# Two MLPs by seven products: where a group's first copy-out and three of its sums stand in the queues of ScalarE and VectorE

## The chip, the core and the metric

The kernel runs on one core of a Trainium2 chip. The metric is the device time of one execution in microseconds (us), the median of several runs; smaller is better.

## The reference, cut to what matters

Two layers over 512 tokens of width 1024, all in float32. Layer 0 mixes with stick-breaking attention, layer 1 with a gated linear recurrence; behind each mixer stands an MLP. The change touches the two MLPs alone:

```python
D_MODEL, SEQ, D_FF = 1024, 512, 4 * 1024

def squared_relu_mlp(h, w1, w2):
    u = jax.nn.relu(h @ w1)          # 512 x 1024 by 1024 x 4096: "up"
    return (u * u) @ w2              # 512 x 4096 by 4096 x 1024: "down"

for layer in range(2):
    x = x + mixer(rms_norm(x, norm_mix[layer]))
    x = x + squared_relu_mlp(rms_norm(x, norm_mlp[layer]), mlp_w1[layer], mlp_w2[layer])
return rms_norm(x, norm_final)
```

## The kernel before, in words

**Operands.** Every float32 operand of a matrix product is cut into two halves of a shorter format, and TensorE multiplies three times (high by high, low by high, high by low). The high half is a cast on ScalarE (`wh` for weights, `bh` and `sh` for activations, 128x1024 a weight block), the low half the difference between raw data and high half, a subtraction on VectorE (`wl`, `bl`, `sl`). So each weight block costs a DMA, a cast on ScalarE and a subtraction on VectorE before TensorE may use it.

**Seven products.** The hidden width of 4096 is taken in four quarters `q4` = 0 to 3. Quarter 0's upward product is done plainly (`squared`). From quarter 1 on the upward product is done in two groups `p` = 0 and 1, each a 2x2 block product with seven block products in place of eight, in the order P1, P5, P6, P3, P7, P2, P4; the downward product of a quarter has the same seven, twice each (`g` = 0 and 1). One product of one group is a step; a loop of a quarter has 28 steps, 14 upward and 14 downward. An upward step is 24 matmuls of 256 columns, a downward step 12 of 512.

Four of the seven need a sum of two weight blocks: VectorE adds for P5 and P6 (`b<-b,b`), a DMA of GpSimd that adds while it writes does it for P7 and P4 (line 1053). P3's weights are a plain block (`b22`).

**Banks.** An upward group sums in three banks of PSUM: P1, P6, P7 and P4 in the first, P5 and P3 in the second, P2 in a third. A partial sum has to be copied out by ScalarE before the next product adds to that bank: P1's copy (`u<-ps_...`, COPY) stands between P1 and P6, which are two steps apart, P5's between P5 and P3. The copies, combined on VectorE, become the four blocks of `u`. After relu and square, `split` cuts them into halves, and `sums` makes four sums of the four blocks, each from the one before, for the downward products.

**Order.** TensorE's order is the list of steps. ScalarE's and VectorE's work of the MLPs is held to the order in which the code records it (`Ordered`): between step `i` and step `i + 1` stands `leave(i)`, the work that follows product `i`, and in it `prepare(i + 4)`, which makes the weights' halves for a later step (`make`, `operand`). There are four buffers for `wh` and `wl`, taken in turn. `operand`, `sums`, `split` and `leave` record through `self.A` (ScalarE) and `self.V` (VectorE); all these instructions carry the helper's line, L765, in the profile. Matmuls of upward steps are L976, of downward ones L1071.

When an upward group's P1 is about to run, the step before it, which is P4 of the group before (a downward one for `p` = 0, the upward group 0 for `p` = 1), calls `prepare` for this group's P3. So the halves of P3's weights are recorded ahead of the copy of P1. Behind P4 of group 0, relu and square of the last block come first, then P3's halves, then

```python
                elif name == "P4":
                    self.sums(p, slice(0, 2))
```

Of the kernel before, what the change touches and what calls it, by code (L numbers as in the profile page):

```python
# [61 lines left out]
def hybrid_encoder(  # L62
# [234 lines left out]
    def home_tile(tag, n, name):  # L297
        return home.tile([P, S], F32, tag=tag, name=name, bufs=n)

    with ExitStack() as actx:  # L300
# [4 lines left out]
        later = sp.tile([P, S], F32, tag="later", name="later")  # L305
# [94 lines left out]
        sums = hp.tile([P, S], F32, tag="early", name="ssq")  # L400
        odd = hp.tile([P, S], F32, tag="ks", name="odd", bufs=1)
        sqs = [sums, odd, *(sc[:, :S] for sc in scans)]
        sqs += [work.tile([P, S], F32, tag=tag, name="sq") for tag in ("sq", "sq", "r")]
        others = {getattr(mybir.EngineType, e) for e in ("Activation", "DVE", "Pool", "SP")}
        with tc.manual_schedule(engines=others):
# [14 lines left out]
            for kind, c in START:  # L420
                if kind == "x":
                    halves("mix0", c, xcs[c])
                elif (kind, c) == ("q", 0):
                    parts[0][3](c, None)
                elif kind != "s":
                    parts["qknm".index(kind)][3](c)
                else:
                    A.activation(sqs[c], xcs[c], AF.Square)
                    if c:
                        V.tensor_tensor(sums, sums, sqs[c], ALU.add)  # L430
# [268 lines left out]
        steps = chain(*(g for g, _ in fill))  # L699
# [6 lines left out]
        for i in range(n_fill):  # L706
# [5 lines left out]
            if i == LATE:  # L712
                x = [home_tile(tag, n, "x") for tag, n in HOMES[:7]]
# [61 lines left out]
    class Mlp:  # L775
# [104 lines left out]
            (2, 3, 2, ALU.subtract), (3, 0, 3, ALU.subtract), (0, 2, 0, ALU.subtract), (1, 0, 1, ALU.add),  # L880
        )

        def sums(self, p, i):

            u = self.u[p]
            for out, x, y, op in self.SUMS:
                self.V.tensor_tensor(u[:, i, out, :], u[:, i, x, :], u[:, i, y, :], op)

        def xa(self, block, k):
# [219 lines left out]
        def run(self, first, between, end):  # L1109
# [5 lines left out]
            steps = []  # L1115
# [5 lines left out]
            units, ws, sums, us = {("down", 0): first}, {}, {}, {}  # L1121

            def place(i):

                return (i + self.STEPS // 2) % self.STEPS
# [8 lines left out]
            def add(i, ahead=1):  # L1134

                if i >= len(steps) or i in done or steps[i][3] not in ("P5", "P6"):
                    return
                *what, name = steps[i]
                far = what[0] == "down" and (name, what[2]) in FARS
                if ahead > (5 if far else 2 if name == "P5" else what[0] == "up"):  # L1140
                    return
                if steps.index((*what, {"P5": "P1", "P6": "P5"}[name])) in made:
                    done.add(i)

                    self.added(unit(i), name, far=far)

            def make(i):
                if i >= len(steps):
                    return
                name = steps[i][3]  # L1150
                kind, q4, p, name = steps[i]
                at = 0
                if kind == "up":
                    at = self.OPEN_AT if (p, name) == (0, "P1") else UP_AT
                ws[i] = made[i] = self.operand(self.source(unit(i), name), at)

                for before, x in (("P5", "P7"), ("P6", "P4")):
                    if name == before:
                        self.added(unit(i), x)

            def prepare(i):

                if i < len(steps) and steps[i][0] == "up":

                    if steps[i][3] == "P7" or self.layer and steps[i][1:] == (1, 0, "P4"):
                        return
                if i - 1 in range(len(steps)) and i - 1 not in made and i > 2:
                    make(i - 1)
                if i < len(steps) and steps[i][0] == "down":
                    add(i, 0)  # L1170
                    if waiting and place(i) in (20, 22, 23):
                        self.split_slot(*waiting.pop(0))
                make(i)
                for n in range(i + 1, i + 6):
                    add(n, n - i)

            def last_sums(u, which):
                for to, a, b, how in which:
                    self.V.tensor_tensor(u[to], u[a], u[b], how)

            def load(i):
# [18 lines left out]
                elif at == 25 and q4 < NQ - 1:  # L1200
                    self.load(units["up", q4 + 1], (1, "b12"), (1, "b22"))

            def leave(i):

                ahead = i + 4
                if i < 0:
                    return
                kind, q4, p, name = steps[i]
                bank = sums[kind, q4, p if kind == "up" else 0][self.PRODUCTS[name][3]]
                if kind == "down":  # L1210
                    if p:
                        for n in range(2):
                            self.collect(name, n, bank[n])
                    prepare(ahead)
                    if q4 == 0:

                        k = {19: 2, 20: 2, 24: 3, 25: 3}.get(place(i))
                        if k:
                            (self.sums_of_x if place(i) in (19, 24) else self.halves_of_sums)(k)
                        if place(i) == 26:  # L1220
                            self.replace()
                    return
                u, three = us[p], bank.rearrange("p (i n) -> p i n", i=2)
                keep = {"P1": 0, "P6": 1, "P5": 2, "P7": 3}.get(name)
                if keep is not None:

                    self.A.copy(u[keep], three)
                at, x, y, op = {
                    "P3": (1, three, u[1], ALU.subtract),
                    "P7": (2, u[2], u[3], ALU.subtract),  # L1230
                    "P2": (0, u[0], three, ALU.add),
                    "P4": (3, three, None, None),
                }.get(name, (None,) * 4)
                if op:
                    self.V.tensor_tensor(u[at], x, y, op)
                if name == "P4":
                    self.A.activation(u[3], three, AF.Relu)
                    self.square(u[3])
                    if p:
                        last_sums(u, self.SUMS[:2])  # L1240
                if later:
                    later.pop()()
                prepare(ahead)
                if op:
                    def rest(u=u, at=at):
                        self.A.activation(u[at], u[at], AF.Relu)
                        self.square(u[at])
                        if p:
                            self.split_slot(p, u[at], at)

                    if p and name == "P3":
                        later.append(rest)
                    else:
                        rest()
                    if name == "P2" and not p:
                        self.split(p, slice(0, 2), slice(0, 3), slice(0, 3))
                elif name == "P4" and p:
                    last_sums(u, self.SUMS[2:3])
                    self.split_slot(p, u[2], 5)
                    last_sums(u, self.SUMS[3:])  # L1260
                    waiting[:] = [(p, u[j], 3 + j) for j in (0, 1, 3)]
                elif name == "P4":
                    self.sums(p, slice(0, 2))
                elif name in ("P5", "P6") and p:
                    n = ("P5", "P6").index(name)
                    self.split(0, n, slice(0, 4), slice(3, 7))

            waiting, later = [], []
            make(0)
            add(1)  # L1270
            make(1)
# [11 lines left out]
            for i, (kind, q4, g, name) in enumerate(steps):  # L1283
                load(i)
                leave(i - 1)
                if i == len(steps) - 2:
                    break
                if kind == "down":
                    self.part(sums.setdefault((kind, q4, 0), {}), name, g, ws.pop(i))
                    continue  # L1290
                if name == "P1":
                    us[g] = self.slots_of(g)
                banks = sums.setdefault((kind, q4, g), {})
                to = self.PRODUCTS[name][3]
                new = to not in banks
                if new:
                    banks[to] = self.bank()
                self.up(name, ws.pop(i), banks[to], new)
# [492 lines left out]
```

## Time and profile before

| | |
|---|---|
| median of 3 runs | 1037.46 us (1037.34 to 1038.66) |
| the profiled execution's own time | 1038.87 us |
| its span, first to last instruction | 1037.2 us |
| mean granted TensorE clock | 0.999 |
| busy: TensorE matmul, weight loads | 1023.4 us, 890.5 us |
| busy: VectorE, ScalarE, GpSimd | 858.2 us, 701.7 us, 172.3 us |

In the profile's names PE is TensorE's matmuls, PEld its weight loads, DVE VectorE, ACT ScalarE, POOL GpSimd, SP the queue that issues most DMAs. Each row of a timeline gives the start in us from the span's start, the time that the row took, engine, line, operation, output and input tiles; in square brackets stands the idle time of the engine before it and what ended it. Matmuls overlap, so that a matmul's own time is longer than the spacing of their starts; gaps are read from starts and from the weight loads' waits. The layers' MLP loops lie at about 290 to 563 us and 757 to 1030 us of the span.

### The profile page before, as it was taken

To read this page: it belongs to the slowest core of one execution; us is meant where nothing else is said; L and a number is where in the kernel's file an instruction comes from. 1 tells how busy PE (TensorE), PEld (TensorE's weight loads), DVE (VectorE), ACT (ScalarE), POOL (GpSimd) and SP (SyncE) were. 2 spreads that over 40 slices of the span, in tenths; PEclk is the share of its full clock that TensorE was granted. 3 is DMA by queue.
4 is the path that set the end of the run, shared out by engine and by line. 5 is a ranking of instruction groups with operands and counts; after the bars stand their busy time and mean duration, and the time that the engine had idled before them with its cause. 6 is when DMAs were issued, how large, how long until landed. Compare 5 with 4: busy or idle time off the path is not lost.

```text
span 1037.2 us, 15857 instructions
## 1 busy us (share of the span) xinstructions
PE 1023.4 (99%) x5862; PEld 890.5 (86%) x5862; DVE 858.2 (83%) x1148; ACT 701.7 (68%) x1083; POOL 172.3 (17%) x239
## 2 busy tenths in 40 slices
PE   9999999999999999999999999999999999999997
PEld 7888888888888988988988888888888988988986
DVE  7888787848788898898899888984789798898897
ACT  6777676826766773773775799963755773873866
POOL 0444444410010010010011121200010010010013
PEclk9999999999999999999999999999999999999999
DMA  7745454528546667667682575452446667677653
GB/s 244 208 120 143 121 149 103 164 85 299 137 79 189 178 139 203 170 135 207 166 209 77 153 190 143 102 223 89 94 75 173 176 146 198 166 146 197 156 124 112
DMA packets 53260, 160.46 MB, mean 155 GB/s; under 512 B 6720, under 2 KB 8256, under 8 KB 53184
## 3 DMA queue, kind: packets, MB, share of 16 engines
q1 hardware_dynamic: 42096, 120.35, 35.6%
q0 software_dynamic: 10656, 38.80, 22.6%
q8 instruction: 46, 0.75, 0.3%
q10 hardware_dynamic: 432, 0.31, 0.1%
q14 instruction: 30, 0.25, 0.1%
HBM read 137.41 MB, written 4.19 MB: 137 GB/s over the span
## 4 chain that ended last, share of the span: by engine, by line
PE 67%; DVE 14%; ACT 11%; issue 4%; DMA 3%; SPq 0%; POOL 0%; ACTq 0%; DVEq 0%; POOLq 0%
PE ps_t L1071 10%; DVE wl L765 6%; PE ps_acc L1071 5%; PE ps_acc L231 5%; PE ps_acc L229 5%; PE ps_acc L230 5%; ACT wh L765 4%; PE ps_acc L976 4%; ACT u L765 3%; DVE b L765 3%; PE ps_t L231 2%; PE ps_t L230 2%; PE ps_t L229 2%; PE ps_z L976 2%; PE ps_z L1071 2%
## 5 line engine op out<-in xcount | busy, mean ns | idle before, releaser
L765 ACT CAST wh<-b 128x1024 fp32r<-128x1024 f32 x168 | 174.2, 1049 | 125.1 <-DVE b L765 79.7
L765 DVE TENSOR_TENSOR wl<-b,wh 128x1024 fp32r<-128x1024 f32 x168 | 203.8, 1222 | 46.4 <-ACT wh L765 46.1
L1053 POOL DMA_DIRECT2D b<-in_w_dn x40 | 34.9, 874 | 364.1 <-DVE b L765 269.7
L229 PE MATMUL ps_acc<-xgh,wh 128*128 128x512 f32 x192 | 78.5, 409 | 0.0
L231 PE MATMUL ps_acc<-xgl,wh 128*128 128x512 f32 x192 | 75.2, 392 | 0.0
L230 PE MATMUL ps_acc<-xgh,wl 128*128 128x512 f32 x192 | 75.1, 391 | 0.0
L224 DVE TENSOR_TENSOR wl<-raw,wh 128x512 fp32r<-128x512 f32 (+2 forms) x70 | 61.2, 901 | 15.0 <-ACT wh L222 15.0
L589 DVE TENSOR_TENSOR_SCAN scan<-keep,later 128x128 f32<-128x128 f32 (+1 forms) x64 | 58.9, 924 | 17.1 <-ACT keep L579 9.7
L765 ACT ACTIVATE u<-u 128x512 f32<-128x512 f32 x100 | 63.1, 632 | 8.9 <-DVE u L765 7.3
L222 ACT CAST wh<-raw 128x512 fp32r<-128x512 f32 (+2 forms) x70 | 50.7, 759 | 20.8 <-PE ps_acc L231 7.3
L593 POOL TENSOR_TENSOR w<-w,scan 128x128 f32<-128x128 f32 (+1 forms) x64 | 51.5, 807 | 56.2 <-DVE scan L589 52.6
L1053 POOL DMA_DIRECT2D b<-in_w_up x24 | 20.8, 867 | 238.2 <-DVE b L765 70.7
L765 DVE TENSOR_TENSOR b<-b,b 128x1024 f32<-128x1024 f32 x48 | 58.7, 1223 | 1.3
L765 DVE TENSOR_TENSOR u<-u 128x512 f32<-128x512 f32 (+1 forms) x92 | 54.9, 597 | 2.7 <-ACT u L765 1.1
L765 ACT CAST wh<-raw 128x1024 fp32r<-128x1024 f32 x46 | 48.1, 1047 | 8.4 <-PE ps_acc L1071 8.3
L976 PE MATMUL ps_z<-xgh,wh 128*128 128x256 f32 x192 | 53.1, 277 | 0.0
L976 PE MATMUL ps_z<-xgh,wl 128*128 128x256 f32 x192 | 53.1, 277 | 0.0
L976 PE MATMUL ps_acc<-low,wh 128*128 128x256 f32 x192 | 53.0, 276 | 0.0
L1071 PE MATMUL ps_t<-wl,sh 128*128 128x512 f32 x126 | 49.8, 395 | 1.1 <-DVE wl L765 1.0
L1071 PE MATMUL ps_t<-wh,bh 128*128 128x512 f32 x126 | 49.2, 391 | 0.0
L1071 PE MATMUL ps_t<-wh,sl 128*128 128x512 f32 x126 | 49.1, 390 | 0.0
L1071 PE MATMUL ps_t<-wh,sh 128*128 128x512 f32 x126 | 49.1, 390 | 0.0
(399 smaller groups left out, 3410.7 us busy)
## 6 DMA issues: line engine op xcount, KB each, us to landing
b<-in_w_dn SPq DMA_DIRECT2D x48, 512.0 KB, 4.4
b<-in_w_dn POOLq DMA_DIRECT2D x40, 512.0 KB, 5.7
b<-in_w_up SPq DMA_DIRECT2D x36, 512.0 KB, 4.6
b<-in_w_up POOLq DMA_DIRECT2D x24, 512.0 KB, 5.5
raw<-in_w_m SPq DMA_DIRECT2D x16, 512.0 KB, 4.4
raw<-in_w_dn SPq DMA_DIRECT2D x16, 512.0 KB, 4.6
raw<-in_w_in SPq DMA_DIRECT2D x16, 512.0 KB, 3.8
raw<-in_w_qk SPq DMA_DIRECT2D x12, 512.0 KB, 3.9
```

The lines of the kernel that those rows point to most:

```text
L222: A.copy(wh[:, k, :], raw[:, k, :])
L224: V.tensor_tensor(wl[:, k, :], raw[:, k, :], f(wh[:, k, :]), ALU.subtract)
L229: PE.matmul(ps, wh, ah, start=start, stop=False)
L230: PE.matmul(ps, wl, ah, start=False, stop=False)
L231: PE.matmul(ps, wh, al, start=False, stop=stop)
L589: V.tensor_tensor_scan(sc[:, S - n : S][:, ::-1], keep[:, :n][:, ::-1], later[:, S - n :][:, ::-1], 1.0, ALU.mult, ALU.max,)
L593: G.tensor_tensor(wt, wt, sc[:, S - n + 1 : S + 1], ALU.mult)
L765: ins = getattr(self.e, name)(*args, **kwargs)
L976: PE.matmul(ps[:, i * HS : (i + 1) * HS], m, y, start=new and i == k == n == 0, stop=i == 1 and k == C // 2 - 1 and n == 2, skip_group_che ...
L1053: G.dma_start(out=unit[b].rearrange("p j n -> p (j n)"), in_=unit["src"](to), accum_op=ALU.add)
L1071: PE.matmul(ps, m, y[:, jj, cols], start=first and n == 0, stop=last and n == 2, skip_group_check=not new,)
```

## The change

In `leave`, the `prepare` that comes right before an upward P1 is held back (`held`) until the next `leave`, that of P1 itself, and runs there behind P1's copy. So ScalarE's copy of P1 stands in front of the cast for P3's high half, in both groups of the three quarters that have them, in both layers. Behind P4 of group 0 only the first of the four sums is recorded at its old place; the other three come in P1's `leave` of group 1, behind P3's low half. No instruction is added or taken away.

```diff
-        def sums(self, p, i):
+        def sums(self, p, i, of=slice(4)):
 
             u = self.u[p]
-            for out, x, y, op in self.SUMS:
+            for out, x, y, op in self.SUMS[of]:
                 self.V.tensor_tensor(u[:, i, out, :], u[:, i, x, :], u[:, i, y, :], op)
...
+            def prepare_or_hold(i):
+
+                if i + 1 < len(steps) and steps[i + 1][0] == "up" and steps[i + 1][3] == "P1":
+                    held.append(i + 4)
+                else:
+                    prepare(i + 4)
+
             def leave(i):
...
                 if kind == "down":
...
-                    prepare(ahead)
+                    prepare_or_hold(i)
...
                     self.A.copy(u[keep], three)
+                if held:
+                    prepare(held.pop())
+                    if p:
+                        self.sums(0, slice(0, 2), slice(1, 4))
...
-                prepare(ahead)
+                prepare_or_hold(i)
...
                 elif name == "P4":
-                    self.sums(p, slice(0, 2))
+                    self.sums(p, slice(0, 2), slice(1))
```

The next two pieces are of the last quarter of layer 0 (quarter 3), where its upward group 1 begins. The first is ScalarE's queue; `ps_z` and `ps_o` are the banks of P1 and P5, `b_5311` the weights of P3.

```order
 L765 ACTIVATE u<-ps_acc 128x2x256
 L765 ACTIVATE u<-u 128x2x256
+L765 COPY u<-ps_z 128x512
 L765 CAST wh<-b_5311 128x1024
-L765 COPY u<-ps_z 128x512
 L765 COPY u<-ps_o 128x512
 L765 CAST wh<-b_5309 128x1024
```

P1's copy has changed places with the cast for P3; relu and square of group 0's last block ahead of them, and P5's copy and P7's cast behind them, stand where they stood.

The second is VectorE's queue at the same place; `bl<-u,bh` is the low half of group 0's first three blocks, `b_5309` and `raw` are the weights of P7 and P2.

```order
 L765 TENSOR_TENSOR wl<-b_5255,wh 128x1024
 L765 TENSOR_TENSOR bl<-u,bh 128x2x768
+L765 TENSOR_TENSOR u<-u 128x2x256
 L765 TENSOR_TENSOR wl<-b_5311,wh 128x1024
-L765 TENSOR_TENSOR u<-u 128x2x256 x4
+L765 TENSOR_TENSOR u<-u 128x2x256 x3
 L765 TENSOR_TENSOR wl<-b_5309,wh 128x1024
 L765 TENSOR_TENSOR wl<-raw,wh 128x1024
```

One sum has gone in front of P3's low half, three have stayed behind it.

The third is ScalarE's queue at the beginning of group 0 of the same quarter; `b_5249` is the block whose last cast here is for P6, `b_5253` are the weights of P3, `b_5251` those of P7; both `ps_acc` are banks, the first with P1's sum, the second with P5's.

```order
 L765 CAST wh<-b_5249 128x1024 x3
+L765 COPY u<-ps_acc 128x2x256
 L765 CAST wh<-b_5253 128x1024
-L765 COPY u<-ps_acc 128x2x256 x2
+L765 COPY u<-ps_acc 128x2x256
 L765 CAST wh<-b_5251 128x1024
 L765 CAST wh<-raw 128x1024
```

Here, too, P1's copy has changed places with P3's cast; VectorE's and GpSimd's queues are as before at this place. On SP's queue two loads that are not weights (`x` in layer 0, the final norm's factors in layer 1) have moved ahead of one load of downward weights in the last quarter of each layer.

More of the change, by code (lines that the diff above doesn't have):

```diff
@@ L1201, in load @@
                     self.load(units["up", q4 + 1], (1, "b12"), (1, "b22"))
+            def prepare_or_hold(i):
[3 more added lines that the diff above has]
+                    prepare(i + 4)
             def leave(i):
-                ahead = i + 4
                 if i < 0:
@@ L1266, in leave @@
                     self.split(0, n, slice(0, 4), slice(3, 7))
-            waiting, later = [], []
+            waiting, later, held = [], [], []
             make(0)
```

## The prediction

> **What bounds the kernel now.** I read the page first, then the waits of TensorE's weight loads over the whole span, then the timelines around one site, then busy times by stretch, and last VectorE's waits behind the site. The page gives the span and the busy shares:
>
> ```profile
> span 1037.2 us, 15857 instructions
> PE 1023.4 (99%) x5862; PEld 890.5 (86%) x5862; DVE 858.2 (83%) x1148; ACT 701.7 (68%) x1083; POOL 172.3 (17%) x239
> ```
>
> TensorE has work nearly all the time, so what can be won lies in its stalls. The waits of its weight loads name them (total us, times, longest):
>
> ```profile
> PEld ps_z L976 <- ACT u L765: 3.8, 6, 1.8
> PEld ps_t L1071 <- DVE wl L765: 3.5, 6, 0.7
> PEld ps_z L1071 <- DVE wl L765: 2.5, 7, 0.5
> PEld ps_acc L1071 <- DVE wl L765: 2.0, 6, 0.3
> ...
> PEld ps_acc L976 <- ACT u L765: 0.6, 1, 0.6
> ```
>
> Rows one and five are the upward steps (L976): seven waits for ScalarE's copy of a partial sum, 3.8 + 0.6 = 4.4 us. Rows two to four are the downward steps (L1071): 19 waits for VectorE's low halves of weights, 3.5 + 2.5 + 2.0 = 8.0 us. The change goes at the first kind. The question is what then becomes of the second.
>
> One site, group 1 of layer 0's last quarter: the last load of P5 and the first of P6.
>
> ```profile
> 509.42 0.19 PEld L976 LDWEIGHTS ps_o<-low,wh 128*128 128x128 f32 x1
> 509.89 0.19 PEld L976 LDWEIGHTS ps_z<-bh,wh 128*128 128x128 f32 x1 [0.29 <-ACT u L765]
> ```
>
> ScalarE there: cast for P3, copies of P1 and P5, cast for P7.
>
> ```profile
> 508.33 1.04 ACT L765 CAST wh<-b 128x1024 fp32r<-128x1024 f32 x1
> 509.26 0.58 ACT L765 COPY u<-ps_z 128x512 f32<-128x512 f32 x1
> 509.84 0.59 ACT L765 COPY u<-ps_o 128x512 f32<-128x512 f32 x1
> 510.32 1.06 ACT L765 CAST wh<-b 128x1024 fp32r<-128x1024 f32 x1
> ```
>
> VectorE there: low half of three blocks, low half of P3's weights, the four sums, low half of P7's; and the fourth sum by itself.
>
> ```profile
> 507.30 1.76 DVE L765 TENSOR_TENSOR bl<-u,bh 128x1536 fp32r<-128x1536 f32 x1 [1.49 <-ACT bh L765]
> 509.40 1.23 DVE L765 TENSOR_TENSOR wl<-b,wh 128x1024 fp32r<-128x1024 f32 x1 [0.34 <-ACT wh L765]
> 510.54 2.87 DVE L765 TENSOR_TENSOR u<-u 128x512 f32<-128x512 f32 x4
> 513.32 1.22 DVE L765 TENSOR_TENSOR wl<-b,wh 128x1024 fp32r<-128x1024 f32 x1
> ...
> 512.71 0.69 DVE L765 TENSOR_TENSOR u<-u 128x512 f32<-128x512 f32 x1
> ```
>
> In an unbroken run P6's first load would stand some 0.11 us behind P5's last, at 509.53. But its bank is free only when P1's copy ends, 509.26 + 0.58 = 509.84, and it loads at 509.89: 0.36 us lost. The copy is late because ScalarE casts P3's weights first, from 508.33.
>
> Busy time ahead of and in the stretch from here to the last downward stall (length, then PE, PEld, DVE, ACT, POOL):
>
> ```profile
> 502.00:509.00 7.00, 7.00 (x64) 7.00 (x64) 4.91 (x5) 5.49 (x8) 0.88 (x1) 1.00 0.57 92
> 509.00:541.00 32.00, 31.70 (x201) 27.69 (x199) 30.08 (x36) 23.29 (x32) 3.48 (x4) 1.00 0.82 215
> ```
>
> From 509 to 541 VectorE is busy 30.08 of 32 us, 94%, against 4.91 of 7, 70%, ahead of it. Its idle times from 513 to 541:
>
> ```profile
> DVE sl L765 <- ACT sh L765: 0.6, 1, 0.6
> DVE wl L765 <- ACT wh L765: 0.6, 1, 0.6
> DVE u L765 <- ACT u L765: 0.2, 1, 0.2
> ```
>
> None waits for TensorE. The end of the stretch shows the kind, on ScalarE, VectorE and the weight loads:
>
> ```profile
> 538.68 2.00 ACT L765 CAST wh<-b 128x1024 fp32r<-128x1024 f32 x2 [4.78 <-DVE b L765]
> 539.77 2.36 DVE L765 TENSOR_TENSOR wl<-b,wh 128x1024 fp32r<-128x1024 f32 x2 [0.57 <-ACT wh L765]
> 541.04 0.19 PEld L1071 LDWEIGHTS ps_t<-wl,sh 128*128 128x128 f32 x1 [0.67 <-DVE wl L765]
> ```
>
> VectorE adds, ScalarE, which has waited 4.78 us for that add, casts, VectorE subtracts, and TensorE, which has waited 0.67, loads. So from P7's low half at 513.32 to TensorE's stall at 541.04 VectorE sets the pace, with short calls on ScalarE. TensorE gets free of it only there. **What bounds this part of a loop is VectorE's chain and not the stall at P6.** A microsecond taken from P6's stall is waited out again below, unless the chain itself starts earlier.
>
> **The change, part by part.**
>
> *The copy in front, group 1.* P1's copy would start when the work before it has let ScalarE go, at 508.33, and end at 508.33 + 0.58 = 508.91, before P5's last load: this site's stall is gone. The longest, 1.8 us, and the 0.6 of row five lie in the two groups of layer 1's first quarter, where ScalarE is later still. The copy comes forward by one cast, 509.26 - 508.33 = 0.93 us, so the 0.6 goes, TensorE then arrives at the 1.8 earlier by as much, and 1.8 + 0.6 - 0.93 = 1.5 us stay. Of 4.4 us 2.9 vanish. By themselves they are worth nothing, as long as VectorE's chain covers them.
>
> *P3's halves behind it.* A cast behind a copy starts 510.32 - 509.84 = 0.48 after it: 508.33 + 0.48 = 508.81, done at 508.81 + 1.05 = 509.86. VectorE's subtraction now starts 0.03 behind the cast's end (508.33 + 1.04 against 509.40), so then at 509.89, and ends at 511.12. A product takes 2.73 us (the two copies of group 0 below, 488.07 and 490.80, each wait for the end of one), so P3 begins at about 509.53 + 2.73 = 512.26: 1.1 us of cover. P5's copy has to wait for P5 and stays at 509.84, P7's cast at 510.32, so nothing behind moves on ScalarE.
>
> *The sums.* VectorE idles 0.34 us ahead of P3's low half now. Then it has longer to wait, and one sum fits in: the 1.76 us row ends at 509.06, the sum takes 0.69 and is done by 509.8. From 509.89 on: low half to the next start 510.54 - 509.40 = 1.14, to 511.03; two steps from one dependent sum to the next of (512.71 - 510.54) / 3 = 0.72, to 512.47; last sum to next start 513.32 - 512.71 = 0.61, to 513.08. **P7's low half starts at 513.08 in place of 513.32, 0.24 us earlier**: the 0.72 of a sum taken off the path, less the 0.49 by which P3's low half is later. All of the chain follows, down to the stall at 541.04. TensorE arrives there 0.36 us earlier and waits the difference longer.
>
> *Group 0.* ScalarE is not late there (first its row, then VectorE's):
>
> ```profile
> 484.44 2.00 ACT L765 CAST wh<-b 128x1024 fp32r<-128x1024 f32 x2 [2.66 <-DVE b L765]
> 488.07 0.59 ACT L765 COPY u<-ps_acc 128x512 f32<-128x512 f32 x1 [1.64 <-PE ps_acc L976]
> 490.80 0.59 ACT L765 COPY u<-ps_acc 128x512 f32<-128x512 f32 x1 [2.14 <-PE ps_acc L976]
> ...
> 487.98 1.22 DVE L765 TENSOR_TENSOR wl<-b,wh 128x1024 fp32r<-128x1024 f32 x1
> 492.36 1.23 DVE L765 TENSOR_TENSOR wl<-b,wh 128x1024 fp32r<-128x1024 f32 x1 [3.17 <-ACT wh L765]
> ```
>
> Now both casts run ahead and ScalarE idles 1.64 us until P1 ends. Then P3's cast waits for P1 too: copy at 488.07, cast at 488.55, low half from 489.63 to 490.86 in place of 487.98. VectorE's next work starts at 492.36, 1.5 us of cover; P3 begins at about 490.6 + 2.73 = 493.3, 2.4 us of cover for TensorE. I cost it at nothing; if the cover were gone, P3 would start later by what is over. The stall of 0.6 us that goes is in a group 0, but behind it ScalarE waits for a DMA (2.6 us, below), so nothing of it passes on.
>
> *DMAs.* P3's raw block is read longer, so its reload starts 1.65 us later in group 0 and 0.5 in group 1. These are downward weights, used only in the next steps, and no wait for one stands among the waits of TensorE or VectorE above. The two loads that pass one downward load on SP's queue come in the last quarter, cost it an issue each, and I take zero. ScalarE's waits for the adding DMAs bound it:
>
> ```profile
> ACT wh L765 <- DMA b<-in_w_up: 3.5, 2, 2.6
> ```
>
> Two waits, 0.9 and 2.6 us. A reload that shares the engines with the awaited block and starts 0.5 us later may bring it up to half of that, 0.25 us, sooner, or change nothing.
>
> *Sum.* Six chains (three quarters, two layers) by 0.24 make 1.44 us. The profiled execution took 1038.87 us, its span and 1.67 us around it, and would take 1037.4. The runs' median is 1.41 us below it, so the forecast is 1037.46 - 1.44 = **1036.0 us**. Bounds: if a cast starts only when the copy before it has ended (0.58 in place of 0.48), a chain gains 0.14, in all 0.84; with the DMA's 0.25 it is 1.7. With half a us of scatter to each side (the three runs lie within 1.3) this case reaches from 1035.2 to 1037.2. About 0.2%, 2.1 us, is what a measurement of this kernel can tell from no change; the forecast lies inside that.
>
> **The rivals.**
>
> *The vanished stall is won.* If the downward stalls don't take it back, the 2.9 us are the gain: 1034.6 us. For it speaks the page's 99% of TensorE; against it the 19 waits for VectorE and the 94% of the stretch that decides. The Trainium skill (Perfetto Trace Analysis, Identifying the Most-Contended Engine and Optimization Strategy) looks for the engine with the highest occupancy, judges TensorE by its weight loads, and closes that engine's gaps; by it over the whole span (86% against VectorE's 83%) the change would be worth the gaps it closes, 1034.6. The page adds that the engine may change from stretch to stretch, and the trace agrees with that: from 509 to 541 the weight loads have 27.69 of 32 us, 87%, VectorE 94%. Chance 0.12.
>
> *Nothing moves.* If P3's low half starts so late that it eats all of the sum's 0.72 us, which takes ScalarE 0.24 us more than the rows say, P7's low half stays at 513.32 and the time at 1037.5; the stalls only move down. Chance 0.16.
>
> *Slower: TensorE in a slow spell behind a stall.* In layer 0's first quarter the stall before P6 is 0.8 us, and behind it TensorE issues more slowly than at the same place of the next quarter; the third row stands behind the stall of 1.8 us (PE busy, granted clock, DMA):
>
> ```profile
> PEld ps_z L976 <- ACT u L765: 0.8, 1, 0.8
> ...
> 357.50:367.50 10.00, 10.00 (x87) 1.00 0.55 181
> 435.50:445.50 10.00, 10.00 (x91) 1.00 0.53 172
> 823.50:833.50 10.00, 10.00 (x91) 1.00 0.66 205
> ```
>
> 87 matmuls in 10 us against 91, 4.4% less, at the same granted clock. It costs nothing where VectorE's chain covers it. The change makes the stalls at the chain's end longer, by 0.1 us in most loops and more in the first quarters, and behind those nothing covers TensorE. A spell of five products there costs 5 x 2.73 x 0.044 = 0.6 us; with one in each of six loops 3.6 - 1.44 = 2.2 us are lost: 1039.6. It decides if stalls of about 0.8 us bring it on. Against it speaks the third row. [...] Chance 0.10.
>
> **How the numbers follow.** The forecast has 0.62. A sixth of it, 0.10, lies below 1035.4; with the first rival's 0.12 that makes 0.22 for faster by over 0.2%. Two thirds of the last rival, 0.07, are slower by over 0.2%, and 0.71 is left within 0.2%. The range holds the forecast, the second rival with its scatter, and most of the first: 1034.4 to 1037.9.
>
> **What would show it.** Right: weight loads of L976 wait for ScalarE's copies at one place only, layer 1's first quarter, about 1.5 us; the waits for VectorE's `wl` in the downward steps grow from 8.0 to about 10 us; in group 1 the second sum starts 1.14 us behind P3's low half, P7's low half some 0.24 us earlier behind the 1.76 us row. Wrong: with downward waits still at 8.0 us the first rival holds; with P7's low half no earlier the second; with fewer matmuls in the 10 us behind a stall the third.

## The result, and the profile after

The changed kernel takes **1035.74 us** (median of 14 runs, 1035.07 to 1037.35), the kernel before 1038.02 us in the runs beside it (14 runs, 1036.21 to 1039.03). The ratio is 0.9979, 95% interval 0.9971 to 0.9986: 2.2 us faster, 1.5 to 3.0. Forecast were 1036.0 us, as 1.44 us less than before. The gain is some 0.8 us larger than its terms. That the time itself comes within 0.3 us of the forecast is partly luck: the kernel before was 0.6 us slower in these runs than in the three from which the forecast started.

The page of the kernel after, span and busy times; its own time is 1035.46 us:

```profile
span 1033.7 us, 15863 instructions
PE 1023.5 (99%) x5862; PEld 890.9 (86%) x5862; DVE 859.0 (83%) x1148; ACT 701.7 (68%) x1083; POOL 170.9 (17%) x239
```

Busy times are the same within 1.4 us on every engine; only idle time has gone. The waits of TensorE's weight loads (total us, times, longest):

```profile
PEld ps_t L1071 <- DVE wl L765: 3.5, 6, 0.7
PEld ps_z L1071 <- DVE wl L765: 3.1, 8, 0.5
PEld ps_acc L1071 <- DVE wl L765: 2.5, 7, 0.4
PEld ps_t L1071 <- DVE sl L765: 1.6, 6, 0.4
...
PEld ps_z L976 <- ACT u L765: 0.7, 2, 0.4
```

The upward stalls are down from 4.4 to 0.7 us. The downward waits for `wl` rose from 8.0 to 9.1, and 1.6 for `sl` are new: 10.7 in all. Of 3.7 us of vanished stall 2.7 came back below.

The site of the prediction, group 1 of layer 0's last quarter, on the weight loads, ScalarE and VectorE of the kernel after (start, us):

```profile
508.25 0.19 PEld L976 LDWEIGHTS ps_o<-low,wh 128*128 128x128 f32 x1
508.36 0.19 PEld L976 LDWEIGHTS ps_z<-bh,wh 128*128 128x128 f32 x1
...
507.16 0.57 ACT L765 COPY u<-ps_z 128x512 f32<-128x512 f32 x1
507.63 1.05 ACT L765 CAST wh<-b 128x1024 fp32r<-128x1024 f32 x1
...
506.13 1.76 DVE L765 TENSOR_TENSOR bl<-u,bh 128x1536 fp32r<-128x1536 f32 x1 [1.48 <-ACT bh L765]
507.99 0.69 DVE L765 TENSOR_TENSOR u<-u 128x512 f32<-128x512 f32 x1
508.71 1.23 DVE L765 TENSOR_TENSOR wl<-b,wh 128x1024 fp32r<-128x1024 f32 x1
509.86 2.14 DVE L765 TENSOR_TENSOR u<-u 128x512 f32<-128x512 f32 x3
511.91 1.22 DVE L765 TENSOR_TENSOR wl<-b,wh 128x1024 fp32r<-128x1024 f32 x1
```

P6's first load stands 0.11 us behind P5's last: that stall is gone. P7's low half (last row) starts 511.91 - 506.13 = 5.78 us behind the 1.76 us row; before it was 513.32 - 507.30 = 6.02. **It comes 0.24 us sooner, the size forecast.** The stall at the chain's end, here and one quarter earlier, and the stretch between:

```profile
462.13 0.19 PEld L1071 LDWEIGHTS ps_t<-wl,sh 128*128 128x128 f32 x1 [0.63 <-DVE wl L765]
539.63 0.19 PEld L1071 LDWEIGHTS ps_t<-wl,sh 128*128 128x128 f32 x1 [0.64 <-DVE wl L765]
...
507.64:539.64 32.00, 31.79 (x203) 27.73 (x202) 30.32 (x36) 23.54 (x32) 3.48 (x4) 1.00 0.84 218
```

In the kernel before the first of these loads stood at:

```profile
463.34 0.19 PEld L1071 LDWEIGHTS ps_t<-wl,sh 128*128 128x128 f32 x1 [0.67 <-DVE wl L765]
```

From stall to stall a loop took 541.04 - 463.34 = 77.70 us before and 539.63 - 462.13 = 77.50 after. VectorE is busy 30.32 of 32 us there, 95%. The four loops of the second and third quarters each became 0.21 to 0.29 us shorter (from one downward matmul to the same one a quarter later, in the two traces). Layer 0's first quarter became 0.71 shorter and **layer 1's first quarter 1.43**. The surplus is there.

It is in a wait that the prediction had quoted, ScalarE's for group 0's adding DMA. GpSimd's issue of it and the cast that waits, kernel before, then kernel after:

```profile
800.84 0.87 POOL L1053 DMA_DIRECT2D b<-in_w_up  x1 [6.94 <-DVE wl L765]
807.67 2.00 ACT L765 CAST wh<-b 128x1024 fp32r<-128x1024 f32 x2 [2.56 <-DMA b<-in_w_up]
```

```profile
799.38 0.87 POOL L1053 DMA_DIRECT2D b<-in_w_up  x1 [6.94 <-DVE wl L765]
805.03 2.00 ACT L765 CAST wh<-b 128x1024 fp32r<-128x1024 f32 x2 [2.05 <-DMA b<-in_w_up]
```

From issue to cast it is 6.83 us before and 5.65 after: 1.2 us less, and the loop's chain starts sooner by that.

### The profile page after: what moved, and what is told of

Same layout as the page of the kernel before. It is cut to its first block, busy times and chain, and to the rows that moved or that the text cites. A ratio compares the mean times of both kernels' runs of the same rounds, so it can differ in the third digit from the quotient of the medians.

```text
span 1033.7 us, 15863 instructions
## 1 busy us (share of the span) xinstructions
PE 1023.5 (99%) x5862; PEld 890.9 (86%) x5862; DVE 859.0 (83%) x1148; ACT 701.7 (68%) x1083; POOL 170.9 (17%) x239
## 4 chain that ended last, share of the span: by engine, by line
PE 76%; DVE 12%; ACT 7%; issue 3%; DMA 1%; DVEq 0%; ACTq 0%; POOL 0%; POOLq 0%
PE ps_t L1071 10%; PE ps_acc L976 7%; DVE wl L765 5%; PE ps_acc L229 5%; PE ps_acc L231 5%; PE ps_acc L230 5%; PE ps_acc L1071 5%; PE ps_z L976 3%; ACT wh L765 3%; ACT u L765 3%; PE ps_t L229 2%; PE ps_z L1071 2%; PE ps_t L231 2%; PE ps_t L230 2%; DVE b L765 2%
```

## The experiments

The theory is that of the prediction: a loop is as long as VectorE's chain behind P7's low half makes it. The rival is that TensorE's stall before P6 counts by itself. The measured time alone can't tell them apart, as the rival's 2.9 us lie within its interval of 1.5 to 3.0. A second question came with the result: why the adding DMA of layer 1's first quarter landed sooner. "By ratio" below is the ratio less 1, times the median of before beside it; the interval of each ratio is about ±0.9 us, ±1.2 us for the kernels with five runs.

**The halves of the change.** *Copy alone* has the whole change but leaves all four sums behind P3's low half.

```diff
-                        self.sums(0, slice(0, 2), slice(1, 4))
+                        self.sums(0, slice(0, 2))
...
-                elif name == "P4":
-                    self.sums(p, slice(0, 2), slice(1))
```

> ScalarE's half of the change alone: P1's copy in front of the cast for P3, VectorE's order as before (P3's low half, then all four sums). Theory (VectorE's chain sets a loop): P3's low half starts about 0.49 us later and nothing is put in front of it, so P7's low half comes 6.49 us behind the start of the 1.76 us row in place of 6.02, 0.47 later, and each of six loops is longer by that: 2.8 us slower than before, at most 0.5 us of it given back by an adding DMA in the first quarters; TensorE's waits for the copies before P6 are gone all the same. Rival (the stall at P6 is what is won): as fast as the whole change or faster, 2.3 to 3.7 us below before.

It took 1040.37 us (11 runs) against 1038.60 (23): ratio 1.0017 [1.0009, 1.0026], 1.8 us **slower**. VectorE at the site:

```profile
507.01 1.76 DVE L765 TENSOR_TENSOR bl<-u,bh 128x1536 fp32r<-128x1536 f32 x1 [1.48 <-ACT bh L765]
509.59 1.23 DVE L765 TENSOR_TENSOR wl<-b,wh 128x1024 fp32r<-128x1024 f32 x1 [0.82 <-ACT wh L765]
510.73 2.87 DVE L765 TENSOR_TENSOR u<-u 128x512 f32<-128x512 f32 x4
513.52 1.22 DVE L765 TENSOR_TENSOR wl<-b,wh 128x1024 fp32r<-128x1024 f32 x1
```

VectorE now idles 0.82 us ahead of P3's low half in place of 0.34, and P7's low half is 513.52 - 507.01 = 6.51 us behind the split, 0.49 later than before. The four steady loops are 0.43 to 0.50 us longer. The stall before P6 is gone at five of six sites, but TensorE's upward stalls as a whole are not (their sum over the run; then ScalarE and the weight loads at the site):

```profile
PEld ps_z L976 <- ACT u L765: 4.1, 7, 1.0
...
513.63 1.05 ACT L765 CAST bh<-u 128x1024 fp32r<-128x1024 f32 x1 [1.59 <-DVE u L765]
514.59 0.57 ACT L765 COPY u<-ps_z 128x512 f32<-128x512 f32 x1
515.22 0.19 PEld L976 LDWEIGHTS ps_z<-xgh,wh 128*128 128x128 f32 x1 [0.46 <-ACT u L765]
```

Six of the seven now stand before P7, two products on. P7 has to wait for the copy of P6's sum, and that copy stands behind a cast that has waited 1.59 us for VectorE's sums. So VectorE's chain, which is later here, holds TensorE already at P7. The copy in front moved TensorE's gap instead of closing it, opened one on VectorE, and cost time by that.

*Sums alone* leaves ScalarE's order as it was and puts one sum ahead of P3's low half in group 1.

```diff
...
+                if name == "P4" and not p:
+                    self.sums(p, slice(0, 2), slice(1))
                 prepare(ahead)
...
-                    self.sums(p, slice(0, 2))
+                    self.sums(p, slice(0, 2), slice(1, 4))
```

> VectorE's half alone: one sum in front of P3's low half, three behind it, ScalarE's order as before (cast for P3, then P1's copy). Theory: P7's low half 1.86 + 0.62 + 1.14 + 2 x 0.72 + 0.61 = 5.67 us behind the start of the 1.76 us row in place of 6.02, 0.35 earlier; 6 x 0.35 = 2.1 us faster than before, though TensorE's 4.4 us of waits before P6 stay as they are. Rival: no gain, within 0.5 us of before, since the waits before P6 stay.

1036.45 us (12 runs), ratio 0.9981 [0.9972, 0.9990], 2.0 us faster, with the upward stalls still there:

```profile
PEld ps_z L976 <- ACT u L765: 3.1, 6, 1.6
...
PEld ps_acc L976 <- ACT u L765: 0.6, 1, 0.6
```

So 3.7 of the 4.4 us of stall stay and nearly the whole gain is there. With 4.1 us of upward stall one kernel is slower than before, with 3.7 us the other is faster: the rival falls with these two.

**The chain by itself.** *Sum less* is the kernel before with the last of the four sums left out in the last three quarters of each layer.

```diff
...
-                    self.sums(p, slice(0, 2))
+                    self.sums(p, slice(0, 2), slice(3))
```

> The kernel before, in which the last of group 0's four sums is left out in quarters 1 to 3 (its block enters the downward product unsummed); every order is as before. Theory: VectorE's chain is 0.72 us shorter in each loop, 6 x 0.72 = 4.3 us faster than before, with the waits before P6 unchanged at 4.4 us. Rival: no change, within 0.5 us.

1034.63 us (5 runs), ratio 0.9961 [0.9950, 0.9973], 4.1 us by ratio; four steady loops each 0.67 to 0.78 us shorter, a sum's 0.72. What is taken off VectorE in front of P7's low half comes off the loop, one for one.

**More sums ahead.** *Two ahead* and *three ahead* are the change with two and with three sums in front of P3's low half.

```diff
-                        self.sums(0, slice(0, 2), slice(1, 4))
+                        self.sums(0, slice(0, 2), slice(2, 4))
...
-                    self.sums(p, slice(0, 2), slice(1))
+                    self.sums(p, slice(0, 2), slice(2))
```

> The whole change with two sums in front of P3's low half and two behind, in place of one and three. Theory: VectorE has no idle time left here, P7's low half 1.86 + 0.72 + 0.61 + 1.14 + 0.72 + 0.61 = 5.66 us behind the 1.76 us row's start (the change: 5.78), so 0.12 us a loop or 0.7 us below the change. Rival: the same time as the change, as the stall at P6 is gone in both.

> The whole change, but three sums in front of P3's low half and one behind it. Theory (VectorE's chain): VectorE does the same work without a gap, so P7's low half starts as in the kernel with two ahead, 0.35 to 0.4 us per loop earlier than before: 1035.5 us, ratio 0.997. But P3's low half now ends at about 512.4 in the times of the site, 0.1 to 0.5 us after TensorE wants it, so TensorE gets a new stall before P3 in up to six loops, 0.6 to 3 us in sum; by the theory it costs nothing, as the downward stalls shrink by as much. Rival (TensorE's own stalls count): slower than with two ahead by 0.6 to 3 us.

The diff is that of two ahead. Two ahead: 1035.52 us (5 runs), ratio 0.9969 [0.9957, 0.9980]. Three ahead: 1034.97 us (5 runs), ratio 0.9961 [0.9948, 0.9973], **the fastest that keeps all four sums**; the two can't be told apart by their intervals. VectorE with two ahead:

```profile
505.54 1.76 DVE L765 TENSOR_TENSOR bl<-u,bh 128x1536 fp32r<-128x1536 f32 x1 [1.49 <-ACT bh L765]
507.40 1.42 DVE L765 TENSOR_TENSOR u<-u 128x512 f32<-128x512 f32 x2
508.74 1.22 DVE L765 TENSOR_TENSOR wl<-b,wh 128x1024 fp32r<-128x1024 f32 x1
509.87 1.41 DVE L765 TENSOR_TENSOR u<-u 128x512 f32<-128x512 f32 x2
511.20 1.22 DVE L765 TENSOR_TENSOR wl<-b,wh 128x1024 fp32r<-128x1024 f32 x1
```

511.20 - 505.54 = 5.66 us, 0.36 sooner than before and 0.12 sooner than with one ahead: the second sum fills what was left of VectorE's idle time. A third can win no more there, and with three the same two rows stand 511.65 - 505.99 = 5.66 apart. The stall it was to cause at P3 is in the weight loads' waits, at two places and not at six:

```profile
PEld ps_o L976 <- DVE wl L765: 0.8, 2, 0.6
```

It cost nothing that can be seen, as the theory says; the rival wanted at least 0.6 us more than with two ahead. With intervals of ±1.2 us on both kernels this is weak evidence by itself.

**One group at a time.** *Group 0 alone*, *group 1 alone* and *first hold* limit the copy in front to group 0, to group 1 (with the sums), and to group 0 of the first quarter of each layer. The diff is first hold's condition, against the changed kernel; in it and in group 0 alone the four sums stand as before.

```diff
-                if i + 1 < len(steps) and steps[i + 1][0] == "up" and steps[i + 1][3] == "P1":
+                if i + 1 < len(steps) and steps[i + 1][0] == "up" and steps[i + 1][1:] == (1, 0, "P1"):
...
```

> The copy of P1's sum goes in front of P3's halves in group 0 alone; group 1 and the four sums stand as before. Theory (VectorE's chain): group 0's halves have 1.5 us of cover, so the chain of a loop starts where it did, 0.0 us in the four later loops. What is open is the wait for the adding DMA of P4's weights in the first quarters, which the change shortened by 0.5 us (layer 0) and 1.2 us (layer 1) in its trace. If the copy in front brings that DMA sooner, this kernel is 0.8 to 1.7 us faster than before (ratio 0.9984 to 0.9992) and its landing in layer 1's first quarter takes about 5.6 us in place of 6.8. If the difference was scatter of one execution: 0.0 us, ratio 1.000, landing anywhere from 5.6 to 7.

> The copy in front and the sums behind P3's low half in group 1 alone; group 0 as before. Theory (VectorE's chain, 0.24 us per loop): 1.4 us faster than before, ratio 0.9986, and the adding DMA in layer 1's first quarter as slow as before. If the change's whole gain comes from group 1: 2.3 us faster, ratio 0.9978. If the stall before P6 alone counted, the same 2.9 us less as the whole change by that theory, ratio 0.9972.

> The copy in front in group 0 of the first quarter of each layer alone, all else as before. If the copy in front there is what brings the adding DMA sooner, it has the whole gain of the kernel with the copy in front in all groups 0, 0.8 to 1.7 us, ratio 0.9984 to 0.9992. If it is scatter, or comes from elsewhere: 0.0 us, ratio 1.000.

Group 0 alone: 1037.54 us (11 runs), 0.9988 [0.9979, 0.9997]. Group 1 alone: 1036.49 (11), 0.9980 [0.9971, 0.9989], an interval that holds all three of its stated outcomes. First hold: 1036.76 (11), 0.9983 [0.9974, 0.9991]. So the copy in group 0, which the chain prices at nothing and whose four steady loops moved by 0.05 us at most, wins 1.3 to 1.8 us, and it wins them in a first quarter. Group 0 alone missed its stated landing, though: the adding DMA took 7.29 us in its trace, an execution of 1039.02 us at the slow end of its runs.

**Why the adding DMA lands sooner.** My first idea was that it shares the DMA engines with the downward loads behind it. *Loads later*, *hold and later* and *three and later* hold two of these loads, and the raw block behind them, until it has landed; they start from the kernel before, from first hold and from three ahead.

```diff
+                    if (self.layer, q4) == (1, 1):
+                        old = units["up", q4][0]
+                        for tag in ("b22", "b12"):
+                            seen = small.tile([P, 1], F32, tag="seen", name="seen")
+                            G.tensor_tensor(seen, old[tag][:, 0, :1], old["b11"][:, 0, :1], ALU.add)
                     self.load(units["down", q4], (0, "b11"), (0, "b12"), (1, "b11"))
```

> The kernel before; in layer 1's first quarter alone two downward loads and the raw block behind them on SP's queue wait until group 0's adding DMA for P4 has landed (two one-column adds on GpSimd that read its block hold them back). In the traces so far the adding DMA there took 5.4 to 5.8 us in five kernels and 6.5 to 7.6 in five others, and the loop's chain started 1.0 to 1.4 us earlier in the first five; these loads are issued 2.1 to 4.5 us behind it. Theory (they share its DMA engines, and the spread is how they share): it now takes 5.3 to 5.6 us, ScalarE's wait there falls from 2.6 to about 1.3 us, and the kernel is 1.0 to 1.3 us faster than before, ratio 0.9988. Rival (the spread has another cause): it takes 5.4 to 7.6 us as before, ratio 1.000, or above it if the held loads come late for the downward steps.

> The same loads held, with the copy in front in group 0 of the first quarters (which alone gave a ratio of 0.9983). If that copy wins because the adding DMA lands sooner, the two don't add up: ratio 0.998 to 0.999, the same as with the loads held alone, within 0.5 us. If it wins elsewhere, they do: 0.997, 2.5 to 3 us faster than before.

> The kernel with three sums ahead, with the same loads held. Its own trace already had the adding DMA at 5.5 us, so by the theory little is left: 0 to 0.5 us faster than three ahead, about 1034.7 us, ratio 0.996. If the loads come late for the downward steps: slower than three ahead by what TensorE then waits.

Medians of 11 runs each: 1039.00 us, 1.0009 [1.0000, 1.0018]; 1038.33 us, 1.0008 [1.0000, 1.0017]; 1035.97 us, 0.9984 [0.9975, 0.9992]. In the trace of loads later the DMA still took 6.48 us, with first hold's copy 5.83, with three ahead's 5.71. The idea falls. Hold and later is as slow as loads later, as its first case said, but slower than the 0.998 to 0.999 stated with it. The queues' packets while it ran, loads later (packets, MB, share of 16 engines):

```profile
q0 software_dynamic: 141, 0.52, 78.4%
q8 instruction: 1, 0.02, 1.8%
```

No packet of the loads' queue (q1) is left in it, and it was late all the same. What is left beside it is one packet of q8. The same stretch, 1.6 to 5.4 us behind the issue, in the kernel before and in the kernel after, and the microsecond ahead of it in the kernel after:

```profile
q0 software_dynamic: 140, 0.52, 86.9%
q1 hardware_dynamic: 23, 0.09, 9.1%
q8 instruction: 1, 0.02, 1.6%
```

```profile
q0 software_dynamic: 141, 0.51, 87.4%
q1 hardware_dynamic: 30, 0.12, 11.5%
...
q0 software_dynamic: 3, 0.01, 9.3%
q8 instruction: 1, 0.02, 5.5%
```

The packet is taken to be a fetch of TensorE's instructions: 46 of them in a run, of 16 KB, 101 to 152 matmuls and about as many weight loads apart, while the other engines' counts between two vary by three times and more. In the thirteen traces below it takes 0.9 to 1.3 us, against mostly 0.3 us for a 4 KB packet of the adding DMA, and in the kernel before the last two packets of the adding DMA start 0.4 and 0.8 us behind all others. By traces:

| kernel | fetch behind the DMA's issue, us | DMA took, us | loop of layer 1's first quarter, us against before |
|---|---|---|---|
| before | 4.1 | 6.76 | 0 |
| sums alone | 3.9 | 6.51 | -0.57 |
| sum less | 4.2 | 7.63 | +1.91 |
| group 1 alone | 4.0 | 7.35 | +0.40 |
| loads later | 3.4 | 6.48 | -0.25 |
| after | 0.8 | 5.57 | -1.43 |
| copy alone | 0.8 | 5.80 | -0.50 |
| two ahead | 0.8 | 5.37 | -1.73 |
| three ahead | 0.9 | 5.54 | -1.59 |
| first hold | 0.7 | 5.63 | -1.12 |
| hold and later | 0.8 | 5.83 | -0.88 |
| three and later | 0.9 | 5.71 | -1.36 |
| group 0 alone | 0.8 | 7.29 | +1.13 |

Its packets run from 1.6 us on. With the copy in front in that group the fetch is over, or nearly, by then; without it the fetch falls among them. Group 0 alone is the exception: an early fetch, and a DMA that was late all the same.

All adding DMAs of the MLP weights, 64 in each of the fourteen traces (fetch moved, below, included), bear this out. With a fetch that starts 1.4 to 4.4 us behind their issue 36 of 40 took over 6.2 us; of the other 856, 14% did. So a fetch is not the only thing that delays them.

*Fetch moved* shifts the fetches and leaves every other engine's order alone: the kernel before with 15 more warm-up matmuls, and all of them narrow.

```diff
-WARM = 7
+WARM = 22
...
-            PE.matmul(warm[:, :P], ones, ones, start=True, stop=True)
+            PE.matmul(warm[:, :8], ones, ones[:, :8], start=True, stop=True)
```

> The kernel before with 15 more warm-up matmuls at its start, all of 8 columns in place of 128: about 30 more matmuls and weight loads in TensorE's instruction stream, so each 16 KB fetch of its instructions should come about 30 matmuls (3.4 us) earlier; ScalarE and VectorE keep their order. In thirteen traces the fetch that meets layer 1's first quarter came 0.7 to 0.9 us behind the issue of group 0's adding DMA in the eight kernels with the copy in front in that group, and 3.4 to 4.2 us behind it, among its packets, in the five others; the DMA then took 5.4 to 5.8 us (once 7.3) against 6.5 to 7.6. Theory (a fetch among the packets delays the DMA): here the fetch falls at about 0.7 us in layer 1's first quarter, the DMA takes 5.4 to 5.8 us in place of 6.8, the loop's chain starts 1.0 to 1.4 us earlier; and it falls at 2.6 us in layer 0's first quarter (6.0 before), where the DMA then takes 6.5 us or more in place of 5.9. Rival (the place of the copy matters in another way): 6.5 to 7.6 us in layer 1 as before, 5.4 to 5.9 in layer 0. The whole time hardly tells: 1.2 won, up to 1 lost, and an unknown change at the start; ratio 0.999 to 1.001.

1044.57 us (5 runs), ratio 1.0063 [1.0050, 1.0077]: the narrow warm-ups took 9.55 us and put the start back by 4.56, a cost that I had left unknown; of the other 2 us some 0.3 lie outside the span, and the rest doesn't show in the trace, itself of 1043.34 us. The fetches shifted by 4.5 and 6.8 us, not by 3.4, but to the sides foreseen. GpSimd's issue and ScalarE's cast in layer 1's first quarter, then in layer 0's, then the queues' packets from 1.4 to 5.3 us behind the latter issue:

```profile
805.84 0.87 POOL L1053 DMA_DIRECT2D b<-in_w_up  x1 [6.94 <-DVE wl L765]
811.65 2.00 ACT L765 CAST wh<-b 128x1024 fp32r<-128x1024 f32 x2 [1.52 <-DMA b<-in_w_up]
...
337.62 0.85 POOL L1053 DMA_DIRECT2D b<-in_w_up  x1 [6.94 <-DVE wl L765]
344.15 2.00 ACT L765 CAST wh<-b 128x1024 fp32r<-128x1024 f32 x2 [1.42 <-DMA b<-in_w_up]
...
q0 software_dynamic: 141, 0.52, 84.0%
q1 hardware_dynamic: 45, 0.18, 12.9%
q8 instruction: 1, 0.02, 2.3%
```

In layer 1 the next fetch is 11.5 us behind the issue; from issue to cast it is 5.81 us in place of 6.83, and the loop is 0.82 us shorter. In layer 0 the fetch is at 1.5 us, and the cast comes 6.53 us behind the issue; before, without a fetch among the packets, it was 6.02:

```profile
333.07 0.85 POOL L1053 DMA_DIRECT2D b<-in_w_up  x1 [6.94 <-DVE wl L765]
339.09 1.05 ACT L765 CAST wh<-b 128x1024 fp32r<-128x1024 f32 x1 [0.91 <-DMA b<-in_w_up]
```

That loop is 0.49 us longer; the four others moved by 0.05 us or less. With ScalarE's order untouched the DMA follows the fetch, in both directions. So, by these traces, **the rest of the change's gain is a collision that it took away by accident.**

The two terms together, six times the mean change of the four steady loops and 1.2 us where the fetch is early (after less before in layer 1's first quarter, less the loop's own 0.26), against the measured times (for group 0 alone the 1.2 is put in although its own trace had the late DMA):

| kernel | steady loop, us | six loops + fetch, us | by ratio, us |
|---|---|---|---|
| after | -0.26 | -1.6 - 1.2 = -2.8 | -2.2 |
| copy alone | +0.47 | +2.8 - 1.2 = +1.6 | +1.8 |
| sums alone | -0.37 | -2.2 | -2.0 |
| two ahead | -0.38 | -2.3 - 1.2 = -3.5 | -3.2 |
| three ahead | -0.39 | -2.3 - 1.2 = -3.5 | -4.1 |
| sum less | -0.74 | -4.5 | -4.1 |
| group 0 alone | -0.02 | -0.1 - 1.2 = -1.3 | -1.3 |
| group 1 alone | -0.28 | -1.7 | -2.1 |
| first hold | -0.04 | -0.2 - 1.2 = -1.4 | -1.8 |

The 1.2 us comes from one pair of traces; over all thirteen, layer 1's first quarter less the steady loop is on average 1.4 us shorter in the eight kernels with the early fetch than in the five others. Every row is within 0.6 us, inside its interval. The three kernels with held loads are not: they are 1.1 to 2.1 us slower than this sum, and their loops' times in the traces don't show where. Among them hold and later has the early fetch and loads later the late one, and their times are the same, so that the 1.2 us can't be seen there.

## Why the prediction was right, and where it was off

- **VectorE's chain sets a loop**: right, and shown by copy alone (stall before P6 gone, loop longer), sums alone (stall there, loop shorter) and sum less (0.74 of 0.72 us). Each step of the site's sum holds within 0.02 us: cast behind copy 0.47 (0.48 forecast), second sum 1.15 behind the low half (1.14), 0.24 us in all.
- **The vanished stall is won**, with "1034.6": fell. The Trainium skill's rule that went with it (Perfetto Trace Analysis, Identifying the Most-Contended Engine and Optimization Strategy: close the gaps of the engine with the highest occupancy) would have made copy alone and sums alone faster by what their upward stalls lost, 0.3 and 0.7 us; measured are 1.8 us slower and 2.0 faster. Its own remark that the engine may change from stretch to stretch is what the runs bear out.
- **"1.5 us stay"** of the stalls, at one place: off. 0.4 us stayed before P6, and another 0.3 stands before P7. The step assumed that ScalarE in layer 1's first quarter is as late as before, but it gets the adding DMA's block 1.2 us sooner.
- **Downward waits "from 8.0 to about 10"**: 10.7 with `sl`. That "TensorE arrives there 0.36 us earlier and waits the difference longer" was wrong about the place: the stall at the chain's end is as long as before (0.64 against 0.67), and the surplus is spread over loads ahead of it.
- **Group 0, "I cost it at nothing ... nothing of it passes on"**: this is the step that failed. ScalarE's and VectorE's rows there moved at no cost, as forecast. But the 0.6 us stall of TensorE that goes in layer 1's group 0 comes with a fetch 3.3 us earlier, and that frees the very DMA which the sentence named as the barrier. The term was costed at 0, with 0.25 us as its bound; it measured 1.2 us in the trace.
- **The bound's mechanism**, a reload that starts 0.5 us later: not it. First hold and hold and later have the early fetch and the short DMA; in layer 1's first quarter no reload moved against the issue in any of the kernels (2.07 us behind it throughout, where not held). In layer 0's first quarter one did start 0.5 us later, 1.90 in place of 1.40 behind the issue, in the eight kernels with the copy in front, and the DMA took 5.3 to 5.7 us in these eight, as in four of the six others.
- **"Nothing moves"** needed P7's low half at its old place; it moved by 0.24 us. **The slow spell** did not come with the change: where 87 matmuls stood in 10 us of layer 0's first quarter, 91 stand now, as its stall is gone too. There it is back in loads later and fetch moved (2.83 us a product against 2.72), and such spells stand in five more traces at other places, in group 0 alone behind a stall of 0.28 us. That loop is 0.02 us longer than before: the spell was covered. What brings it on stays open.
- Layer 0's first quarter gave 0.45 us beyond its chain. All other kernels but copy alone, with its longer chain, and fetch moved have that quarter 0.25 to 1.0 us shorter as well, and but for fetch moved the DMA there took 5.3 to 5.7 us in all of them, against 5.94 in the trace of before. That is scatter of the one execution of before, not the change.

## What to carry to other kernels

Ask for each stall which engine's chain ends last behind it, and price an edit by where it puts the next link of that chain: here a sum moved into VectorE's idle time was the gain, and 3.7 us of TensorE's stalls were worth nothing that the runs can tell. A wait for a DMA is a chain too: before writing that "nothing passes on" because a DMA is awaited behind, list everything that shares its engines, the engines' own instruction fetches included. And a difference of 1 us between two traces can be such a collision; undoing the edit piece by piece tells it from the mechanism that was meant.

## What the runs showed of the hardware

A fetch of TensorE's instructions, one packet of 16 KB, made the adding DMA of 512 KB that it fell into take 6.5 to 7.6 us from issue to landing (five kernels), where without it in seven of eight kernels the same DMA took 5.4 to 5.8; moved by extra warm-up matmuls, it shortened one DMA by 1.0 us and lengthened another by 0.5, against the trace of before. The Trainium skill (Runtime: NRT & Kernel Launch, Instruction fetch mechanics) has each engine fetch its instructions in blocks of 16 KiB by a DMA queue of its own and calls the cost mostly hidden; size and queue agree with the trace, and the cost was 1.2 us where a chain waited for the DMA beside it.

Open are three things: why the fetch comes some 20 matmuls later in the kernels where TensorE waits 0.6 us before P6 in that group, fetch moved aside (most other fetches stay within ten matmuls there, but a few jump by 15 to 40); why the DMA took 7.29 us in group 0 alone, with an early fetch; and why the kernels with held loads are slower than the two terms say, where 0.3 to 0.4 us lie outside the span.
